# A two-layer transformer trunk on one core: the ungated half of the gating layer as seven block products, weight sums by VectorE and by accumulating loads, the second gate block by weight rows

## The chip, the cores and the metric

The kernel runs on one core of a Trainium2 chip. The metric is the device time of one execution in microseconds (us). Before the change three runs gave 1406.53, 1407.19 and 1410.97 us, with a median of 1407.19 us. The engines are named as in the profile: PE (TensorE, matmuls; PEld its weight loads), DVE (VectorE), ACT (ScalarE), POOL (GpSimd) and SP (SyncE, which here only issues transfers).

## The reference, cut to what matters

The input is 512 tokens of width 1024, all in float32. Layer 0 is a chunked attention, layer 1 a gating layer, and each is followed by an MLP. What the change touches is the gating layer and the second product of both MLPs:

```python
def chunked_spatial_gating(h, w_in, v_gain, w_s, b_s, w_out):
    z = jax.nn.gelu(h @ w_in, approximate=False)          # 512x1024 @ 1024x6144
    u, v = jnp.split(z, 2, axis=-1)                       # 512x3072 each
    v = rms_norm(v, v_gain).reshape(B, nw, 128, 8, 384)
    w = jnp.where(mask[None], w_s, 0.0)                   # 8 groups of 128x128
    vm = jnp.einsum('gij,bnjgc->bnigc', w, v) + b_s.T[None, None, :, :, None]
    return (u * vm.reshape(B, S, 3072)) @ w_out           # 512x3072 @ 3072x1024

def squared_relu_mlp(h, w1, w2):
    return jnp.square(jax.nn.relu(h @ w1)) @ w2           # 1024 -> 4096 -> 1024
```

The norm of v needs its sum of squares over all 3072 columns, so no tile can be mixed and gated before the whole gated half v is there.

## The kernel before, in words

A float32 matrix is held as a high and a low part (`Split`, lines 480 to 484: a CAST on ACT at L483 and a subtraction on DVE at L484), and a product is three matmuls, high by high, high by low and low by high (`mm3`, L94; each matmul is recorded at L92). A matmul here takes a 128x128 block as its weights and streams 512 columns of the other matrix into one PSUM bank. Tokens come in four tiles of 128.

Some of the large products are made by a scheme of seven block products (`seven`, L616). Left matrix and weights are cut in 2x2 blocks, 256 tokens by 512 and 512 by 512, and seven products of sums of blocks stand in for eight plain ones. The sums of weight blocks are made on DVE at L631 on whole 512x512 blocks of two 128x1024 tiles; the sums of left blocks at L530; each finished product is added to its output by `put` (for the MLP at L517 and L519, for the gated half at L1425 and L1423). Four weight blocks are loaded per scheme. `Run` (L687) puts the steps in a row: a step's loads are issued `ll` steps and its weight split `lp` steps before its matmuls, (3, 3) in the MLPs and (2, 2) in the gating layer, where a step is 24 matmuls.

The scheme is used three times in each MLP's second product (the last quarter of the 4096 hidden columns is plain, in `project_last`) and twice in the gated half v: columns 0 to 511 (`gate_tile(0, ...)`) and 512 to 1023 (`gate_tile(1, ...)`, the second plain block) are plain, columns 1024 to 3071 are two schemes with `Gate` as output. The finished v goes to DRAM (`v_store`, L1400, issued on POOL) and is loaded again later (`v_load`, L1405).

The ungated half u is plain. `u_block(cb)` (L1518) makes 512 columns for all four token tiles: 24 matmuls a tile, gelu at L1531, v scaled by its row norm and gain at L1533, split at L1535 and L1536, mixed with the 128x128 group matrices by three short matmuls for each group, shifted and multiplied with u at L1549, turned by four 128x128 transposes at L1554 and split again into high and low at L1559 and L1560. Six such blocks alternate with `b_down`, which multiplies a finished block of 512 columns with its rows of `w_out` (96 matmuls, with `wload`, L379, whose split is at L388 and L389) and adds the result to `y` at L517. The last two blocks go through `project_last`, which also adds the residual and starts the norm of the MLP that follows. There `merge` (L498) multiplies y by the adaLN gate at L506, loads the residual `xs` again and adds it at L507.

Pieces of work for later stages (`bg`: rows of the adaLN modulation, mostly L194 on DVE) are spread over the stages by a counter. Buffers are 49 slots of 128x1024 float32 and 8 PSUM banks, handed out in the order in which they came free. Inside `in_order` the code's order is PE's order; outside it a scheduler sets the order on every engine from its own estimate of durations, and each engine then works strictly in its order.

## Time and profile before

| quantity | value |
|---|---|
| median of three runs | 1407.19 us (1406.53 to 1410.97) |
| the profiled execution | 1412.96 us |
| its span, first to last instruction | 1411.2 us |
| busy PE / DVE / ACT / POOL | 1386.7 / 1020.9 / 713.5 / 15.7 us |
| mean granted TensorE clock | 0.993 |

The profile is of one execution. Its span is 1.8 us shorter than its time, and that time is 5.8 us above the median. Busy means that an instruction is on the engine. A busy PE may still be slower than it could be, because matmuls overlap; the pace is read from the number of matmuls that a long stretch holds. An engine's idle time is put down to what ended it.

### The profile page before, as it was taken

Reading aid. Unit: us, or ns where it says so; the run is one execution under the profiler, and the core shown is the slowest. Engines: PE = TensorE matmul, PEld = TensorE weight load, DVE = VectorE, ACT = ScalarE, POOL = GpSimd, SP = SyncE. Lnnn points to the kernel's source line nnn. Section 1 sums busy time; section 2 is a strip of 40 time slices with the busy share of each in tenths; the row PEclk is TensorE's granted clock in tenths of the full one; section 3 lists DMA queues with packets and bytes.
Section 4 is the critical chain, followed back from the end, with each engine's and each line's share of the span. In section 5 each row is a group of like instructions: output and inputs, shape, how many; then the busy total and the mean of one; then the engine's idle time right before and its main releaser. Section 6 shows DMA issues by size and latency. Waiting matters only on the chain.

```text
span 1411.2 us, 18916 instructions
## 1 busy us (share of the span) xinstructions
PE 1386.7 (98%) x7202; PEld 1185.5 (84%) x7202; DVE 1020.9 (72%) x1493; ACT 713.5 (51%) x1231; POOL 15.7 (1%) x46
## 2 busy tenths in 40 slices
PE   8999999899999999999999999999999999999998
PEld 7898888789888888888888888888889988888887
DVE  6889889676667887776995745665677377776883
ACT  6537567655464544537587443233445355453630
POOL 0000000000000000000000000000000000000000
PEclk8999999999999999999999999999999999999999
DMA  9656466573254361356347434435437225242151
GB/s 373 240 144 211 147 194 173 201 264 110 90 169 144 119 224 60 118 197 252 134 147 254 167 106 164 163 127 164 142 113 269 75 87 182 63 147 90 31 164 60
DMA packets 85627, 221.51 MB, mean 157 GB/s; under 512 B 7960, under 2 KB 9376, under 8 KB 85536
## 3 DMA queue, kind: packets, MB, share of 16 engines
q1 hardware_dynamic: 83808, 214.01, 45.9%
q0 software_dynamic: 1728, 6.29, 1.1%
q8 instruction: 56, 0.92, 0.3%
q14 instruction: 35, 0.29, 0.1%
HBM read 197.21 MB, written 14.68 MB: 150 GB/s over the span
## 4 chain that ended last, share of the span: by engine, by line
PE 88%; DMA 6%; DVE 3%; ACT 2%; issue 1%; SPq 0%; POOL 0%; ACTq 0%; POOLq 0%; DVEq 0%
PE p L92 85%; DMA s<-in_ada_w 2%; DMA s<-in_ffn_w 1%; DMA s<-in_a_w_in 1%; DMA s<-in_a_w_out 1%; DMA s<-s 1%; PE p L1554 1%; PE p L1228 1%; PE p L315 1%; DVE s L484 0%; PE p L1139 0%; PE p L920 0%; DVE s L951 0%; ACT s L483 0%; PE p L207 0%
## 5 line engine op out<-in xcount | busy, mean ns | idle before, releaser
L92 PE MATMUL p<-s,s 128*128 128x512 f32 (+2 forms) x6568 | 1323.8, 361 | 9.5 <-DVE nm L1190 2.7
L92 PEld LDWEIGHTS p<-s,s 128*128 128x128 f32 x6568 | 1109.4, 189 | 196.0 <-DVE nm L1190 4.3
L484 DVE TENSOR_TENSOR s<-s,s 128x1024 fp32r<-128x1024 f32 x234 | 280.5, 1222 | 119.1 <-ACT s L483 56.0
L483 ACT CAST s<-s 128x1024 fp32r<-128x1024 f32 x234 | 241.2, 1051 | 166.0 <-PE p L92 109.9
L389 DVE TENSOR_TENSOR s<-s,s 128x1024 fp32r<-128x1024 f32 x80 | 96.7, 1223 | 62.2 <-ACT s L388 50.7
L388 ACT CAST s<-s 128x1024 fp32r<-128x1024 f32 x80 | 83.4, 1052 | 93.8 <-DMA s<-in_b_w_out 34.1
L631 DVE TENSOR_TENSOR s<-s,s 128x1024 f32<-128x1024 f32 x64 | 77.7, 1222 | 33.0 <-DMA s<-in_ffn_w 32.6
L739 ACT ACTIVATE r<-p 128x512 f32<-128x512 f32 x64 | 38.1, 595 | 116.6 <-PE p L92 116.5
L194 DVE SCALAR_TENSOR_TENSOR s<-s,cs,s 128x1024 f32<-128x1024 f32 x70 | 89.7, 1281 | 8.7 <-DMA s<-in_ada_w 7.7
L517 DVE TENSOR_TENSOR s<-p,s 128x512 f32<-128x512 f32 x104 | 70.4, 686 | 19.2 <-PE p L92 18.0
L745 ACT ACTIVATE s<-r 128x256 f32<-128x256 f32 (+1 forms) x112 | 45.0, 443 | 1.2
L424 DVE TENSOR_TENSOR tr<-p,s 128x512 f32<-128x512 f32 (+1 forms) x33 | 22.0, 671 | 30.6 <-PE p L92 30.2
L1195 ACT ACTIVATE s<-s,nm 128x128 f32<-128x128 f32 (+3 forms) x64 | 36.0, 564 | 7.4 <-DVE nm L1190 5.9
L1559 ACT CAST s<-p 128x256 fp32r<-128x256 f32 x48 | 17.7, 370 | 35.5 <-PE p L1554 27.0
L530 DVE TENSOR_TENSOR s<-s,s 128x1024 f32<-128x1024 f32 x28 | 33.6, 1221 | 1.0 <-PE p L92 0.9
L304 ACT ACTIVATE s<-s 128x512 f32<-128x512 f32 x24 | 15.3, 638 | 36.0 <-DVE s L425 34.9
L1233 DVE TENSOR_TENSOR s<-p,s 128x512 fp32r<-128x512 f32 (+3 forms) x64 | 29.3, 484 | 4.0 <-ACT s L1232 3.6
L1560 DVE TENSOR_TENSOR s<-p,s 128x256 fp32r<-128x256 f32 x48 | 20.1, 419 | 16.3 <-ACT s L1559 16.3
L1190 DVE CUSTOM_DVE_ANT_0 s<-p,s 128x128 f32<-128x128 f32 (+3 forms) x64 | 29.6, 485 | 0.9 <-PE p L92 0.8
L1535 ACT CAST s<-s 128x512 fp32r<-128x512 f32 x24 | 14.8, 621 | 27.8 <-DVE s L1533 12.9
L1228 PE MATMUL p<-ident,s 128*128 128x128 f32 x160 | 24.6, 275 | 4.1 <-ACT sq L1310 2.4
L1232 ACT CAST s<-p 128x512 fp32r<-128x512 f32 (+3 forms) x64 | 25.1, 426 | 6.6 <-PE p L1228 5.5
(141 smaller groups left out, 760.9 us busy)
## 6 DMA issues: line engine op xcount, KB each, us to landing
s<-in_ffn_w SPq DMA_DIRECT2D x128, 512.0 KB, 4.5
s<-in_ada_w SPq DMA_DIRECT2D x96, 512.0 KB, 4.9
s<-in_b_w_in SPq DMA_DIRECT2D x48, 512.0 KB, 5.0
s<-in_b_w_out SPq DMA_DIRECT2D x24, 512.0 KB, 4.8
s<-in_a_w_in SPq DMA_DIRECT2D x22, 512.0 KB, 5.2
s<-s SPq DMA_DIRECT2D x64, 128.0 KB, 3.6
vd<-s POOLq DMA_DIRECT2D x12, 512.0 KB, 3.2
s<-vd SPq DMA_DIRECT2D x12, 512.0 KB, 3.4
```

The costliest lines, as they stand in the source:

```text
L92: T.matmul(ps, lhsT, rhs, start=start, stop=stop, skip_group_check=more)
L194: V.scalar_tensor_tensor(acc, r, ck, acc, ALU.mult, ALU.add)
L388: A.copy(hi, raw)
L389: engs[len(ids) // 2 % len(engs)].tensor_tensor(lo, raw, f32(hi), ALU.subtract)
L483: A.copy(self.hi, raw)
L484: mark[0] = V.tensor_tensor(self.lo, raw, f32(self.hi), ALU.subtract)
L517: V.tensor_tensor(dst, ps, dst, ALU.add)
L631: V.tensor_tensor(x[0], y_[0], z[0], ALU.subtract)
L739: A.activation(r, ps, AF.Relu)
L745: A.activation(d, v, AF.Square)
L1195: A.activation(pt[it], pt[it], AF.Exp, bias=nm[:, it:it + 1], scale=-1.0, accum_out=sm[:, it:it + 1])
L1228: T.transpose(ps[:, it * P:(it + 1) * P], b["pt"][it][:, jt * P:(jt + 1) * P], ident)
```

## The change

Five things change.

1. `seven` works in half blocks of weights (256 rows, one 128x1024 tile), so that a scheme is 14 steps of 12 matmuls instead of 7 of 24, and it uses other sums: per scheme seven partial results are put instead of eight, one of them in one go from PSUM (`whole`). Where `near` is false (the MLPs) all sums of weight blocks are made by loads that add (`grow`: a transfer issued on POOL with accumulation, into the tile that held the block before); three blocks are loaded plainly and four are added. Where `near` is true (the gating layer) two sums are made by DVE (`plus`, L628 of the changed kernel) and two by adding loads, and four blocks are loaded plainly.
2. The ungated half u is made by three such schemes (`mix_steps`), 1024 columns each, with `Mix` as output. The mixing and gating of a tile is queued and comes out two steps after its last product (five at the first). The gated tile is turned as before, copied to a full-precision tile, and split in whole 512x256 blocks (`take_parts`).
3. The first 2048 rows of the output product are two plain products of 1024 rows (`down_steps`), walked through by rows of the weights, 24 matmuls a step. The order is u0, down0, u1, u2, down1, and then `project_last` as before.
4. The second plain block of the gated half is four steps of 256 weight rows (`gate_steps`) instead of four token tiles.
5. The row norms of v come from an integer estimate with three refinements on DVE instead of a function on ACT; v is stored by transfers issued on ACT; the last residual is added to y by an adding load on POOL instead of a load and a sum on DVE; `Run` is (4, 4) in the MLPs and (4, 3) in the gating layer, in the smaller steps.

```diff
 
-        def merge(self, xs, g):
...
                 xt[t], xid[t] = self.y[t], self.ids[t]
+                if late:
+                    V.tensor_tensor(xt[t], xt[t], g, ALU.mult)
+                    G.dma_start(xt[t], xs[t], accum_op=ALU.add)
+                    return
                 raw, done = raw_tile([P, D])
                 SP.dma_start(raw, xs[t])
...
             if (t, hf) in self.seen:
-                V.tensor_tensor(dst, ps, dst, ALU.add)
+                V.tensor_tensor(dst, dst, ps, op)
             else:
                 A.copy(dst, ps)
                 self.seen.add((t, hf))
...
-    def seven(left, src, y):
+    def seven(left, src, y, near=False):
+
...
+        def load(name, i, j, s_):
+            raw[name, s_] = t, n = SL.get([P, 2, 512], F32)
+            SP.dma_start(t, block(i, j, s_))
+
+        def grow(i, j, name, s_):
+            G.dma_start(raw[name, s_][0], block(i, j, s_), accum_op=ALU.add)
+
+        def plus(a, b, s_):
+            V.tensor_tensor(raw[a, s_][0], raw[a, s_][0], raw[b, s_][0], ALU.add)
+
+        def right(m, name, add, s_):
+
+            if near and m == 2:
+                plus("x", "w", s_)
+                SL.free(raw["w", s_][1])
+            op[m, s_] = Split(raw[name, s_][0], [P, 2, 512])
+            if near and m == 4:
+                plus("x", "y", s_)
+            if add is None:
+                SL.free(raw[name, s_][1])
+            elif not near or m > 2:
+                grow(*add, name, s_)
+
+        def mult(m, acc, first, outs, done, s_):
+            a, b = left.op[m], op.pop((m, s_))
             for u in range(2):
-                if first:
+                if first and s_ == 0:
...
-                for k in range(4):
-                    bh, bl = b[k // 2].hi[:, k % 2, :], b[k // 2].lo[:, k % 2, :]
-                    mm3(p, a.hi[:, k, c], a.lo[:, k, c], bh, bl, first and k == 0, k == 3, not first)
-                for i, j in outs:
...
+                for k in range(2):
+                    kk = 2 * s_ + k
+                    ah, al, bh, bl = a.hi[:, kk, c], a.lo[:, kk, c], b.hi[:, k, :], b.lo[:, k, :]
+                    mm3(p, ah, al, bh, bl, first and kk == 0, kk == 3, not first)
+                if s_:
+                    for i, j, o, whole in outs:
+                        y.put(2 * i + u, j, p, o, whole)
+                    if done:
+                        PS.free(pi)
+            b.free()
+            if s_:
+                left.done(m)
...
         plan = (
-            (True, ((0, 0),), False),
-            (True, ((0, 0),), True),
-            (True, ((1, 1),), False),
-            (False, ((0, 1),), False),
-            (False, ((0, 1),), True),
-            (False, ((1, 0), (1, 1)), True),
-            (True, ((1, 0),), True),
+            (0, ("x", 0, 0), ("x", (0, 1)), ("z", True, ((0, 0, add, False),), False)),
+            (1, ("z", 1, 0), ("z", None), ("y", True, ((0, 0, add, False),), True)),
+            (2, None, ("x", (1, 1)), ("v", True, ((1, 1, add, False),), False)),
+            (4, ("y", 1, 1), ("y", (0, 1)), ("v", False, ((0, 1, add, False),), True)),
+            (3, None, ("x", (1, 0)), ("z", False, ((0, 1, sub, False),), False)),
+            (5, None, ("y", None), ("z", False, ((1, 1, sub, False),), False)),
+            (6, None, ("x", None), ("z", False, ((1, 0, add, True),), True)),
...
+        def loads(m, b, s_):
+            if near and m == 2:
+                load("w", 0, 1, s_)
+            if b:
+                load(*b, s_)
+
...
     def v_store(cb, b):
 
         v, i = vv.pop((cb, b))
-        G.dma_start(vd[cb, b], v.rearrange("p t n -> p (t n)"))
+        A.dma_start(vd[cb, b], v.rearrange("p t n -> p (t n)"))
...
+    def gate_steps(cb):
...
     def gate_load(cb):
         return wload(b_w_in[0][:, SGH + cb * 512:SGH + cb * 512 + 512], KD)
 
-    steps = []
+    steps = gate_steps(1)
     for p in (1, 2):
-        steps += seven(kept, b_w_in[0][:, SGH + p * 1024:SGH + (p + 1) * 1024], Gate(p))
-    u_ahead = []
-    steps.append(Step(nothing, lambda: u_ahead.append(wload(b_w_in[0][:, 0:512], KD)), nothing, nothing))
...
+    class Mix:
...
+        def put(self, t, hf, ps, op, whole):
+            if (hf, t // 2) not in self.u:
+                self.u[hf, t // 2] = SL.get([P, 2, 512], F32)
+            dst = self.u[hf, t // 2][0][:, t % 2, :]
+            if not whole and (t, hf) not in self.seen:
+                self.seen.add((t, hf))
+                A.copy(dst, ps)
+                return
+            if not whole:
+                V.tensor_tensor(dst, dst, ps, op)
+            A.activation(dst, ps if whole else dst, AF.Gelu)
+            late = 5 if (self.p, hf, t // 2) == (0, 0, 0) else 2
+            later.append((now[0] + late, lambda: self.mix(t, hf, dst)))
+        def mix(self, t, hf, u):
+            cb = 2 * self.p + hf
+            vh = tp.tile([P, 512], F32, tag="tt", name="vh")
+            v, vi = self.v[hf, t // 2]
+            V.scalar_tensor_tensor(
+                vh, v[:, t % 2, :], vr[:, t:t + 1], self.g[:, hf * 512:hf * 512 + 512], ALU.mult, ALU.mult
+            )
+            vs, i = SL.get([P, 2, 512], F32R)
+            A.copy(vs[:, 0, :], vh)
+            V.tensor_tensor(vs[:, 1, :], vh, f32(vs[:, 0, :]), ALU.subtract)
+            ps, pi = bank()
+            c0 = 0
...
+                mark[0] = V.scalar_tensor_tensor(
+                    u[:, c0:c1], ps[:, c0:c1], bsT[:, g:g + 1], u[:, c0:c1], ALU.add, ALU.mult
+                )
...
+    def mix_steps(p):
+        m = Mix(p)
+        out = seven(kept, b_w_in[0][:, p * 1024:(p + 1) * 1024], m, True)
+        out[0].right = then(out[0].right, m.gain, lambda: m.take(0, 0))
+        for i, hf, b in ((6, 1, 0), (8, 1, 1), (10, 0, 1)):
+            out[i].right = then(out[i].right, lambda hf=hf, b=b: m.take(hf, b))
+        return out
+    def down_steps(p):
...
+        def mult(n):
+            hf, j, o = n // 4, 1 - n // 2 % 2, n % 2
+            w = op.pop(n)
+            for t in range(NT):
+                if n % 4 == 0:
+                    ps[t] = bank()
+                a = parts[p, t // 2, j]
+                c = slice(t % 2 * P, t % 2 * P + P)
+                for k in range(2):
+                    kk = 2 * o + k
+                    mm3(
+                        ps[t][0], a.hi[:, kk, c], a.lo[:, kk, c], w.hi[:, k, :], w.lo[:, k, :],
+                        n % 4 == 0 and k == 0, n % 4 == 3 and k == 1,
+                    )
+                if n % 4 == 3:
+                    y.put(t, hf, ps[t][0])
+                    PS.free(ps[t][1])
+            w.free()
+            if n in (5, 7):
+                for i in range(2):
+                    parts.pop((p, i, j)).free()
+            bg((0, 2, 2, 1, 1, 1, 1, 1)[n])
...
+    steps[3].mult = then(steps[3].mult, mixing)
+    steps[-1].mult = then(steps[-1].mult, row_scales)
...
+    u, d = [mix_steps(p) for p in range(3)], [down_steps(p) for p in range(2)]
+    tail = [Step(nothing, down_ahead, nothing, nothing)]
+    for x in u[0] + u[1] + u[2] + d[0] + d[1]:
+        x.mult = then(x.mult, flush)
+    for x, *f in (
+        (u[0][13], take(0, 1)), (d[0][1], take(0, 0)), (u[1][13], last_use), (u[2][11], take(1, 1)),
+        (u[2][13], take(1, 0)), (d[1][1], no_more_mixing), (d[1][4], take(2, 0)), (d[1][5], take(2, 1)),
+    ):
+        x.mult = then(x.mult, *f)
+    steps += u[0] + d[0] + u[1] + u[2] + d[1][:6] + tail + d[1][6:]
...
-        run = Run(steps, 3, 3)
+        run = Run(steps, 4, 4)
...
-    run = Run(steps, 2, 2)
-    run.go()
-    h = kept.only_blocks()
+    run = Run(steps, 4, 3)
+    with tc.issue_after(normed[0].ins):
+        run.prime()
+    keep[0] = 9
+    run.go()
...
-
-    u_block(0)
-    u_block(1)
-    b_down([0])
-    u_block(2)
-    b_down([1])
-    u_block(3)
-    b_down([2])
-    u_block(4)
-    b_down([3])
-    u_block(5)
-    kept.free()
-    SL.free(*[i for _, i in wsT])
-    b_down([4, 5])
+    in_order()
+    g = gbc[1, 2][0]
+    project_last(
+        plain({(i, j): parts[2, i, j] for i in range(2) for j in range(2)}), b_w_out[0][2048:3072, :], g,
+        last.rows, last.cols, lambda: up_ahead(1), y.merge(xs, g, True), spent
+    )
```

On PE, in the middle of the ungated half, before the change: `p_369` and `p_372` are token tiles of a u block, `s_925` is a gated tile being turned, `p_370` is a mixing result, and `s_701` to `s_716` are weights of the block.

```order
L92 MATMUL p_369_8209<-s_917_8143,s_702_6415 128x512
L92 MATMUL p_369_8209<-s_918_8144,s_702_6415 128x512
L92 MATMUL p_369_8209<-s_917_8143,s_703_6416 128x512
L1554 MATMUL p_368_8197<-ident,s_925_8182 128x128
L92 MATMUL p_369_8209<-s_917_8143,s_702_6415 128x512
L92 MATMUL p_369_8209<-s_918_8144,s_702_6415 128x512
L1554 MATMUL p_368_8197<-ident,s_925_8182 128x128 x3
L92 MATMUL p_369_8209<-s_917_8143,s_703_6416 128x512
L92 MATMUL p_370_8240<-s_929_8237,s_841_7498 128x128 x3
L92 MATMUL p_370_8240<-s_929_8237,s_841_7498 128x384 x3
L92 MATMUL p_372_8261<-s_908_8125,s_712_6601 128x512
```

The same place after it: `p_357` and `p_356` are accumulators of one scheme, `p_374` is the first product of the next scheme, and `s_971` is a gated tile.

```order
L92 MATMUL p_357_8295<-s_973_8490,s_779_7038 128x512
L92 MATMUL p_357_8295<-s_974_8491,s_779_7038 128x512
L1602 MATMUL p_369_8581<-ident,s_971_8479 128x128 x2
L1602 MATMUL p_367_8560<-ident,s_971_8479 128x128 x4
L1602 MATMUL p_369_8581<-ident,s_971_8479 128x128 x2
L92 MATMUL p_357_8295<-s_973_8490,s_780_7039 128x512
L92 MATMUL p_374_8699<-s_985_8589,s_694_6389 128x512
```

Before, a tile's 24 matmuls, one transposed tile and one mixing follow each other; now two gated tiles are turned together at the end of a run of matmuls, between the products of two schemes.

On DVE at the same place, before: L389 splits weights, L1560 splits gated tiles, L1549 gates.

```order
L389 TENSOR_TENSOR s_938_8366<-s_936_8363,s_937_8365 128x1024
L1560 TENSOR_TENSOR s_922_8154<-p_368_8197,s_921_8153 128x2x128
L1549 SCALAR_TENSOR_TENSOR s_928_8234<-p_370_8240,bsT,s_928_8234 128x128
L1549 SCALAR_TENSOR_TENSOR s_928_8234<-p_370_8240,bsT,s_928_8234 128x384
L1560 TENSOR_TENSOR s_924_8156<-p_368_8197,s_923_8155 128x2x128
L389 TENSOR_TENSOR s_941_8372<-s_939_8369,s_940_8371 128x1024
```

And after: L628 is the sum of two weight half blocks, L486 the split, L1568 the sum of a product into u, L1595 the gating, L1582 and L1577 the split and the scaling of v.

```order
L628 TENSOR_TENSOR s_967_8465<-s_967_8465,s_984_8587 128x1024
L486 TENSOR_TENSOR s_991_8616<-s_972_8488,s_990_8615 128x1024
L1568 TENSOR_TENSOR s_964_8439<-s_964_8439,p_356_8288 128x512
L1595 SCALAR_TENSOR_TENSOR s_964_8439<-p_370_8636,bsT,s_964_8439 128x384
L1595 SCALAR_TENSOR_TENSOR s_964_8439<-p_370_8636,bsT,s_964_8439 128x128
L1568 TENSOR_TENSOR s_964_8439<-s_964_8439,p_357_8295 128x512
L628 TENSOR_TENSOR s_972_8488<-s_972_8488,s_989_8613 128x1024
L1582 TENSOR_TENSOR s_994_8654<-vh,s_994_8654 128x512
L1577 SCALAR_TENSOR_TENSOR vh<-s_970_8471,vr,s_935_8167 128x512
```

The splits of gated tiles in quarters are gone from between the gating; weight sums and the sums of products into u now stand between the instructions of the mixing.

## Rows read from the trace of the kernel before

**Rows 1.** The page: busy time of the engines in us with the share of the span and the number of instructions, the granted clock in 40 slices of the span, and the chain that ended last by engine.

```profile
PE 1386.7 (98%) x7202; PEld 1185.5 (84%) x7202; DVE 1020.9 (72%) x1493; ACT 713.5 (51%) x1231; POOL 15.7 (1%) x46
...
PEclk8999999999999999999999999999999999999999
...
PE 88%; DMA 6%; DVE 3%; ACT 2%; issue 1%; SPq 0%; POOL 0%; ACTq 0%; POOLq 0%; DVEq 0%
```

**Rows 2.** Busy time in four stretches (us from the span's start): first the length, then busy us and instructions of PE, PEld, DVE, ACT and POOL, then granted clock, DMA share and GB/s.

```profile
700.00:750.00 50.00, 50.00 (x222) 41.30 (x221) 46.30 (x47) 40.39 (x66) 2.96 (x6) 1.00 0.46 153
779.00:1021.00 242.00, 242.00 (x1175) 203.23 (x1174) 149.64 (x227) 87.32 (x140) 0.00 (x0) 1.00 0.44 147
1021.00:1083.20 62.20, 60.42 (x334) 52.02 (x333) 46.34 (x81) 30.48 (x65) 0.00 (x0) 1.00 0.58 206
1083.20:1407.40 324.20, 324.20 (x1588) 275.09 (x1587) 212.41 (x215) 142.02 (x197) 0.00 (x0) 1.00 0.32 101
```

**Rows 3.** PE's groups by shape from 1300 to 1400 us: count, busy us, mean ns of one, idle time before them. Then the first group over the whole span.

```profile
L92 PE MATMUL p<-s,s 128*128 128x512 f32 x439 | 100.1, 389 | 0.0
L92 PE MATMUL p<-s,ones 128*128 128x512 f32 x4 | 1.3, 396 | 0.0
...
L92 PE MATMUL p<-s,s 128*128 128x512 f32 x4648 | 1084.1, 392 | 5.3 <-ACT s L1272 2.1 <-DVE nm L1190 1.4 <-ACT s L980 1.0
```

**Rows 4.** PE in order of time around 812 us: start, length, and what (lengths overlap; the pace is from start to start).

```profile
811.64 0.60 PE L1554 MATMUL p<-ident,s 128*128 128x128 f32 x4
812.00 1.17 PE L92 MATMUL p<-s,s 128*128 128x512 f32 x4
```

**Rows 5.** DVE's groups by shape (count, busy us, mean ns, idle before them): the first two over the whole span, the others from 779 to 1021 us.

```profile
L484 DVE TENSOR_TENSOR s<-s,s 128x1024 fp32r<-128x1024 f32 x234 | 280.5, 1222 | 119.1 <-ACT s L483 56.0 <-PE p L92 52.8 <-issue 4.5
L631 DVE TENSOR_TENSOR s<-s,s 128x1024 f32<-128x1024 f32 x64 | 77.7, 1222 | 33.0 <-DMA s<-in_ffn_w 32.6
...
L194 DVE SCALAR_TENSOR_TENSOR s<-s,cs,s 128x1024 f32<-128x1024 f32 x14 | 17.9, 1282 | 2.8 <-DMA s<-in_ada_w 2.5
L1536 DVE TENSOR_TENSOR s<-s,s 128x512 fp32r<-128x512 f32 x24 | 16.3, 687 | 1.9 <-ACT s L1535 1.7
L517 DVE TENSOR_TENSOR s<-p,s 128x512 f32<-128x512 f32 x24 | 16.2, 685 | 5.2 <-PE p L92 5.2
L1533 DVE SCALAR_TENSOR_TENSOR s<-s,vr,gain 128x512 f32<-128x512 f32 x20 | 14.9, 748 | 14.4 <-PE p L92 11.1 <-issue 1.4 <-PE p L1554 1.1
...
L1549 DVE SCALAR_TENSOR_TENSOR s<-p,bsT,s 128x384 f32<-128x384 f32 x15 | 9.1, 609 | 0.0
L1549 DVE SCALAR_TENSOR_TENSOR s<-p,bsT,s 128x256 f32<-128x256 f32 x16 | 7.0, 479 | 1.0 <-PE p L92 0.8
L1549 DVE SCALAR_TENSOR_TENSOR s<-p,bsT,s 128x128 f32<-128x128 f32 x15 | 5.2, 344 | 0.9 <-PE p L92 0.9
```

**Rows 6.** Transfers. For L625 (half blocks of weights for the schemes), L1400 (stores of v, issued on POOL) and L1405 (their loads back): the issue with its length in ns, least, median and most, and the time to landing. Then the stores of the same size issued on SP, with KB and median us to landing.

```profile
L625 SPq DMA_DIRECT2D s<-in_b_w_in x16: 367/373/642, 619.1 to 719.6; - x16
DMA to landing us min/median/max: 3.4/4.6/11.7
...
L1400 POOL DMA_DIRECT2D vd<-s x12: 531/531/673, 663.0 to 772.2; - x12
DMA to landing us min/median/max: 2.9/3.2/7.6
...
L1405 SPq DMA_DIRECT2D s<-vd x12: 326/338/459, 745.4 to 964.0; - x12
DMA to landing us min/median/max: 3.1/3.4/7.9
...
xs<-s SPq DMA_DIRECT2D x8, 512.0 KB, 2.9
...
xsg<-s SPq DMA_DIRECT2D x4, 512.0 KB, 2.6
```

**Rows 7.** ACT's groups by shape: the first over the whole span, the others from 779 to 1021 us.

```profile
L483 ACT CAST s<-s 128x1024 fp32r<-128x1024 f32 x234 | 241.2, 1051 | 166.0 <-PE p L92 109.9 <-DMA s<-in_ffn_w 28.2 <-DVE s L484 12.6
...
L1531 ACT ACTIVATE s<-p 128x512 f32<-128x512 f32 x24 | 14.4, 600 | 25.7 <-PE p L92 25.7
L1535 ACT CAST s<-s 128x512 fp32r<-128x512 f32 x23 | 14.2, 622 | 27.8 <-DVE s L1533 12.9 <-PE p L92 12.7 <-DVE s L389 2.0
L519 ACT COPY s<-p 128x512 f32<-128x512 f32 x8 | 4.7, 589 | 8.4 <-PE p L92 8.4
```

**Rows 8.** The page: packets and bytes of all transfers.

```profile
DMA packets 85627, 221.51 MB, mean 157 GB/s; under 512 B 7960, under 2 KB 9376, under 8 KB 85536
```

**Rows 9.** The chain that ended last, at the change to the last MLP: start, length, what.

```profile
1019.14 4.40 DMA s<-in_ffn_w
...
1067.88 10.67 DMA s<-in_ffn_w
```

More of the change, by code (lines that the diff above doesn't have):

```diff
@@ L584, in comb @@
             super().comb(d, a, b, o)
+        more = True
         def done(self, m):
-            pass
-        def only_blocks(self):
-            for m in (2, 3, 4, 5):
-                self.op.pop(m).free()
-            return self.rows()
-        def free(self):
-            for x in self.op.values():
-                x.free()
+            if not self.more:
+                super().done(m)
     def plain(p):
@@ L677, in seven @@
+        def loads(m, b, s_):
[3 more added lines that the diff above has]
+                load(*b, s_)
         return [
             Step(
-                (lambda m=m: load(*blocks[m])) if m < 4 else nothing,
-                lambda m=m: right(m),
-                lambda m=m: left.prep(m),
-                lambda m=m: mult(m, *plan[m]),
+                lambda m=m, b=b, s_=s_: loads(m, b, s_),
+                lambda m=m, r=r, s_=s_: right(m, *r, s_),
+                lambda m=m, s_=s_: prep(m, s_),
+                lambda m=m, p=p, s_=s_: mult(m, *p, s_),
@@ L683, in seven @@
             )
-            for m in range(7)
+            for m, b, r, p in plan for s_ in range(2)
         ]
@@ new lines, in then, with both, take_parts @@
+    def then(f, *gs):
+        def both():
+            f()
+            for g in gs:
+                g()
+        return both
+    y = Sum()
+    parts = {}
+    def take_parts(*blocks):
+        for b in blocks:
+            t, n = gated.pop(b)
+            parts[b] = Split(t, [P, 4, 256])
+            SL.free(n)
+    def mix_steps(p):
[5 more added lines that the diff above has]
+        return out
@@ new lines, in trunk_kernel, with down_ahead, last_use, no_more_mixing @@
+    steps[3].mult = then(steps[3].mult, mixing)
+    steps[-1].mult = then(steps[-1].mult, row_scales)
+    def down_ahead():
+        ahead[0] = wload(b_w_out[0][2048:3072, 0:512], KD)
+    def last_use():
+        kept.more = False
+    def no_more_mixing():
+        SL.free(*[i for _, i in wsT])
+    def take(p, j):
+        return lambda: take_parts(*[(p, i, j) for i in range(2)])
+    u, d = [mix_steps(p) for p in range(3)], [down_steps(p) for p in range(2)]
+    tail = [Step(nothing, down_ahead, nothing, nothing)]
```

328 lines of the change are left out of this document (159 added, 169 removed).

## The prediction

> **What bounds the kernel now.** I read the page first. PE is busy for 98% of the span, DVE for 72%, ACT for 51%, POOL for almost nothing, and PE's lines take 88% of the chain that ended last [rows 1]. The granted clock is full in all slices but the first. So the first question is how many matmuls there are. Then I read windows by stage, since busy shares say nothing of the place: from 700 to 750 us (the two schemes of the gated half) and from 779 to 1021 us (the ungated half and most of the output product) PE is never idle [rows 2]; it has idle time, 1.8 us of 62.2, only at the change to the next MLP, 1021 to 1083 us. Because matmuls overlap, "busy" is no proof of full pace, so I counted: 100 us late in the last MLP hold 439 + 4 matmuls of 512 columns, 0.2257 us each [rows 3]; the 50 us of [rows 2] hold 222, which is the same pace. The reader is to see that in the stage that changes most, PE is the limit, and that in the densest window DVE was busy for 46.30 of 50 us and PE still did not wait.
>
> **The matmuls.** The ungated half takes 6 blocks x 4 token tiles x 24 = 576 matmuls of 512 columns now. Three schemes take 3 x 7 products x 2 token tiles x 12 = 504. Everything else on PE keeps its number: the plain part of the output product has 4 x 96 = 2 x 192, the second gate block 96, mixing and transposes the same. So 72 go, at 0.2257 us: **-16.25 us**. They stand in a stretch where PE is the limit, so I count all of it, less what is late next.
>
> **What is late next: DVE in a u scheme.** PE needs 168 x 0.2257 = 37.9 us for its products. Beside it stand eight mixings, which stream three times 512 columns (3 x 0.2257 = 0.68 us), and eight groups of four transposes, 812.00 - 811.64 = 0.36 us each [rows 4]: 8.3 us, together 46.2 us. DVE has, by [rows 5]: 14 weight splits and 4 weight sums at 1.222 (22.0 us); 6 sums of a product into u at 0.685 (4.1); for each of 8 tiles 0.748 for scaling v, 0.687 for its split and 0.609 + 0.344 or 2 x 0.479, so 0.955, for gating (19.1). That is 45.2 us of 46.2, a load of 98%. The schemes u1 and u2 stand in a row, and four gated blocks are split while u2 runs (4 x 1.222 = 4.9): DVE has 95.3 us of work where PE has 92.4. I take the difference, **+2.9 us**. The lower end is 0: the down stages before and after have 8 splits (9.8), at most 8 sums (5.5) and some ten pieces of modulation at 1.28 (L194) beside 192 x 0.2257 = 43.3 us of PE, some 15 us free, into which mixings and splits can move. The upper end: if DVE can be no busier than in the densest window, 92.6%, each scheme lasts 45.2 / 0.926 = 48.8 us, three times 2.6 more, and the four splits 5.3: 13.1 us. I stay near the low end since that window, the nearest row, shows no wait of PE at 93%.
>
> **The adding loads.** The trace has none. The nearest rows are a plain load of the same half block of weights, 4.6 us to landing, a store of such a tile from POOL, 3.2 us, and its load back, 3.4 us [rows 6]. An adding load can't be quicker than the plain one, and if it went like load, read and write in turn it took 4.6 + 3.2 + 3.4 = 11.2 us. I take the plain load and one read of the tile, 7.8 us. The room for it: in the gating layer four steps of 12 matmuls (2.71 us) lie between the split of a tile and the next split of it, 10.8 us, and a split stands three steps ahead of its matmuls, 8.1 us. From 18.9 us go the issue on POOL (0.53), the CAST (1.05) and the subtraction (1.22) of the split [rows 5 to 7], so 16.1 us are left: nothing waits at 7.8 or at 11.2. In an MLP two steps of 24 matmuls lie between as well, and the split is four steps ahead: at least 21.7 + 10.8 - 2.8 = 29.7 us. So 0, and the risk is a rival below. A plain load's slowest landing is 11.7 us, which still fits. POOL gets 72 such issues, 72 x 0.53 = 38 us spread over some 1000.
>
> What speaks against this: the twelve stores issued on POOL landed in 3.2 us at the median, 7.6 at most, while stores of the same size issued on SP took 2.9 and 2.6 [rows 6]; so issuing on POOL cost 0.3 to 0.6 us beside a DVE that was over 90% busy. The Trainium skill says more (SBUF — State Buffer, section "SBUF: two separate sides"): POOL writes the descriptors of its transfers into SBUF itself, and some DVE operations lock it out until they end. By that rule a load would start one DVE operation, 1.22 us, later, or several where they follow without a gap, as in the u schemes. The trace agrees only with the small end. One operation changes no sum, several in a row are what could make the second rival true.
>
> **The rest, each at nothing.** In the MLPs a scheme loses 8 weight sums on DVE (9.8 us) and two sums of results; PE is the limit there too [rows 2], so it gives nothing, and if the cover were gone it would be a gain. The splits of gated tiles at L1559 and L1560 become one copy and whole splits. ACT per u scheme: 14 x 1.05 + 6 x 0.589 + 8 x 0.600 + 8 x (0.622 + 0.589) = 32.7 of 46.2 us [rows 7]; the stores of v that move to ACT's queue add 12 issues of 0.34 us (as SP's loads of v take, [rows 6]). The row norms of v by some 15 short DVE operations are needed only five steps (13.5 us) after the first tile. The last residual: y is scaled (1.22), the adding load is issued (0.53) and lands (7.8 to 11.2), 9.6 to 13.0 us after y; DVE wants it after 42 matmuls and 8 transposes, 10.2 us, and PE only with the transposes another 36 matmuls on. The second gate block by weight rows has the same work. Weights to be loaded grow by 18 blocks of 1.05 MB in the MLPs and 10 in the gating layer, 29 MB on 221.51 [rows 8], 13%, with the DMA engines half idle in these windows. The 1.8 us at the change to the MLP are waits for its weights [rows 9] and stay, within 2 us either way.
>
> **Sum.** The profiled execution took 1412.96 us (span 1411.2 and 1.8 around it): 1412.96 - 16.25 + 2.9 = 1399.6. The median is 5.8 us lower, so **1394 us**.
>
> **Rivals.** First, DVE sets the pace of the u schemes. For it: 98% load, and mixing is a chain DVE-ACT-DVE-PE-DVE-PE in strict queues. Against it: [rows 2]. Price 13.1 instead of 2.9: 1404 us. Second, and slower than before: adding loads land late and splits wait for them on ACT, with evictions and gelu queued behind, for which PE's banks wait. It decides from 16.1 + 13.4 / 5 = 18.8 us to landing, where the five schemes of the gating layer have given back the gain. At twice my upper bound, 22.4 us, each scheme waits 6.3 us, 31.5 in all: 1425 us. For it: nothing in the trace shows an accumulation; against it: 18.8 us is over four plain loads. Third, the change doesn't do what it says: half-size steps double the number of steps, and if PE loses 0.1 us at each of the 70 + 84 steps, 15 us, the time is 1409 with the 2.9. For it: each step waits for its own split; against it: in [rows 4] PE passes from one tile to another without a loss.
>
> **How the numbers follow.** A measurement of this kernel can tell about 0.3%, 4.2 us, from no change: faster is below 1403.0, slower above 1411.4. Forecast 0.60, its own range 1389 (no wait, 1.8 us gained at the change to the MLP) to 1400, all faster. DVE's pace 0.20: 0.10 faster, 0.08 same, 0.02 slower. Late adding loads 0.12: 0.10 slower, 0.02 same. Lost pace 0.08: 0.05 same, 0.03 slower. Together 0.70, 0.15, 0.15. The range that leaves out 2 in 10 is 1388 to 1410.
>
> **What would show it.** PE's 512-column matmuls go from 4648 to 4576 in the group by shape [rows 3], still at about 222 in 50 us. In the u schemes DVE is over 90% busy and PE waits, if at all, for the DVE lines of gating or splits, 3 us in sum. Adding loads land in under 12 us, and ACT's casts do not wait for them. In the MLPs DVE is less busy and PE as full. I am wrong if PE waits more than 8 us between the gate and the next MLP, or if casts wait for weight transfers issued on POOL.

## The result and the profile after

The changed kernel takes 1413.38 us (median of 20 runs, 1408.14 to 1418.41), the kernel before 1408.67 us beside it (20 runs). The ratio is 1.0037, interval 1.0027 to 1.0047: slower, by about as much as can be told from no change, where I had forecast 1394 us. The profiled execution of after took 1416.04 us.

The page of after: busy time, and the chain that ended last by engine and by line. They answer to [rows 1].

```profile
PE 1378.7 (97%) x7130; PEld 1177.0 (83%) x7130; DVE 978.7 (69%) x1422; ACT 744.0 (53%) x1248; POOL 95.0 (7%) x106
...
PE 74%; issue 11%; DMA 7%; DVE 6%; ACT 2%; POOL 0%; SPq 0%; POOLq 0%; DVEq 0%; ACTq 0%
PE p L92 71%; DMA s<-in_b_w_in 2%; DMA vd<-s 1%; DMA s<-xsg 1%; DVE s L958 1%; PE p L1235 1%; DVE s L486 1%; DVE s L1197 1%; DMA s<-s 1%; ACT s L485 1%; DVE s L1240 0%; PE p L1602 0%; DMA s<-in_ada_w 0%; PE p L315 0%; DMA s<-in_x 0%
```

PE has less work and a smaller share of the span, and DVE is less busy than before. In the chain PE fell from 88% to 74%; "issue" has 11% where it had 1, and by line the first thing behind PE is the transfer of weights of the gating layer. Two rows of PE's groups by shape follow, first over the whole span, then from 1300 to 1400 us, to be held against [rows 3].

```profile
L92 PE MATMUL p<-s,s 128*128 128x512 f32 x4576 | 1075.0, 394 | 13.9 <-ACT s L1565 3.6 <-ACT s L1279 2.3 <-DVE s L486 2.2
...
L92 PE MATMUL p<-s,s 128*128 128x512 f32 x439 | 99.8, 389 | 0.0
```

The 72 matmuls are gone, and the pace late in the last MLP is the same to the matmul. So the loss must stand in some stretch. Busy time of after by 25 us (length, then PE, PEld, DVE, ACT, POOL, granted clock, DMA share, GB/s):

```profile
700.00:725.00 25.00, 22.61 (x97) 17.99 (x96) 19.83 (x20) 16.17 (x23) 2.41 (x2) 0.98 0.94 251
725.00:750.00 25.00, 25.00 (x107) 20.60 (x106) 14.76 (x16) 14.20 (x26) 3.61 (x3) 0.95 0.49 120
750.00:775.00 25.00, 23.14 (x94) 18.40 (x93) 14.56 (x14) 14.90 (x24) 1.21 (x1) 0.93 0.92 290
775.00:800.00 25.00, 21.36 (x92) 17.28 (x91) 16.00 (x30) 15.17 (x25) 3.61 (x3) 0.98 0.70 182
800.00:825.00 25.00, 24.19 (x123) 20.55 (x122) 21.32 (x32) 16.22 (x24) 1.20 (x1) 0.95 0.54 146
...
950.00:975.00 25.00, 21.60 (x91) 17.90 (x90) 18.14 (x23) 16.76 (x23) 0.00 (x0) 0.86 0.53 139
...
779.00:1021.00 242.00, 234.15 (x1115) 196.03 (x1114) 185.12 (x240) 132.46 (x184) 14.46 (x12) 0.98 0.61 176
```

Where [rows 2] showed PE busy without a gap at full clock, from the gated half to the output product, it now stops in five of these stretches, and the clock is below full in all six. The waits of PE from 690 to 1000 us (what waited for what, us in total, times, longest):

```profile
PE p L92 <- ACT s L1565: 3.6, 1, 3.6
PE p L92 <- ACT s L1581: 3.4, 2, 2.7
PE p L92 <- DVE s L486: 2.2, 1, 2.2
PE p L92 <- ACT s L485: 1.8, 1, 1.8
PE p L1602 <- DVE s L1595: 0.8, 1, 0.8
```

They add up to 11.8 us. The clock of the six stretches lacks 0.02 + 0.05 + 0.07 + 0.02 + 0.05 + 0.14 = 0.35 of 25 us, 8.8 us. Together 20.6 us against a gain of 16.25: by this estimate the execution should be 4.3 us longer than the 1412.96 of before, and it is 3.1.

DVE is not what PE waits for in the first place, and it was itself idle. What ACT waited for explains more. Two views of line L625 in after from 690 to 1000 us: the adding loads of weights, their issue on POOL (ns, least, median, most), who waited for them, and the time to landing.

```profile
L625 POOL DMA_DIRECT2D s<-in_b_w_in x20: 1203/1203/1467, 695.9 to 946.1; - x20
...
who waited for it (us, times):
  ACT s L485: 34.0, 13
...
DMA to landing us min/median/max: 6.0/8.2/14.5
```

Against [rows 6]: the landing is close to what I took (8.2, taken 7.8), the issue more than twice as long (1.20, taken 0.53), and casts wait for 13 of the 20. One such place in full, the end of the second u scheme: first POOL's issues, then ACT, then PE in order of time (start, length, what, idle time before it and what ended it).

```profile
941.35 2.44 POOL L625 DMA_DIRECT2D s<-in_b_w_in  x2 [49.77 <-ACT s L1565]
944.16 1.20 POOL L625 DMA_DIRECT2D s<-in_b_w_in  x1 [0.38 <-DVE s L486]
946.14 1.20 POOL L625 DMA_DIRECT2D s<-in_b_w_in  x1 [0.77 <-DVE s L486]
```

```profile
947.60 1.05 ACT L485 CAST s<-s 128x1024 fp32r<-128x1024 f32 x1 [3.02 <-DMA s<-in_b_w_in]
...
952.23 1.05 ACT L485 CAST s<-s 128x1024 fp32r<-128x1024 f32 x1 [1.95 <-DMA s<-in_b_w_in]
956.93 1.04 ACT L485 CAST s<-s 128x1024 fp32r<-128x1024 f32 x1 [3.65 <-DMA s<-in_b_w_in]
957.89 0.61 ACT L1581 CAST s<-vh 128x512 fp32r<-128x512 f32 x1
958.41 0.58 ACT L1565 COPY s<-p 128x512 f32<-128x512 f32 x1
958.88 0.62 ACT L1581 CAST s<-vh 128x512 fp32r<-128x512 f32 x1
960.70 2.00 ACT L485 CAST s<-s 128x1024 fp32r<-128x1024 f32 x2 [1.20 <-DMA s<-in_b_w_in]
```

```profile
949.41 6.42 PE L92 MATMUL p<-s,s 128*128 128x512 f32 x27
958.55 0.33 PE L92 MATMUL p<-s,s 128*128 128x128 f32 x1 [2.72 <-ACT s L1581]
959.55 10.56 PE L92 MATMUL p<-s,s 128*128 128x128 f32 x35 [0.68 <-ACT s L1581]
```

Four adding loads, four casts that wait for them, 9.8 us. The first cast is wanted at 947.60 - 3.02 = 944.58, 3.2 us after the issue of its load began. Behind the third stand two casts of scaled v (L1581), with the eviction of a product (L1565) between them, in ACT's strict order, and both stops of PE end with such a cast of v. The last row shows the second price: 35 matmuls, some of them short, take 10.56 us, 0.30 us each, where one of 512 columns took 0.2257 in [rows 3].

The landing is counted from the start of the issue: the last load was issued at 946.14 and landed 14.5 us later, the longest of the 20, and its cast starts at 960.70. The four casts start 3.8 to 4.7 us apart, each as its load lands, and the DMA engines were full meanwhile (DMA share, the last number but one, 0.89 to 1.12 in every 3 us from 943 to 961 us; two of these windows):

```profile
949.00:952.00 3.00, 3.00 (x16) 2.50 (x15) 0.92 (x1) 1.21 (x3) 0.00 (x0) 1.00 1.12 207
952.00:955.00 3.00, 3.00 (x15) 2.45 (x15) 1.23 (x1) 1.05 (x1) 0.00 (x0) 1.00 1.11 257
```

So at this place the later ones shared full engines with the loads before them.

### The profile page after: what moved, and what is told of

It is laid out like the page before. It is cut to its first block, busy times and chain, and to the rows that moved or that the text cites. A ratio compares the mean times of both kernels' runs of the same rounds, so it can differ in the third digit from the quotient of the medians.

```text
span 1414.3 us, 18911 instructions
## 1 busy us (share of the span) xinstructions
PE 1378.7 (97%) x7130; PEld 1177.0 (83%) x7130; DVE 978.7 (69%) x1422; ACT 744.0 (53%) x1248; POOL 95.0 (7%) x106
## 4 chain that ended last, share of the span: by engine, by line
PE 74%; issue 11%; DMA 7%; DVE 6%; ACT 2%; POOL 0%; SPq 0%; POOLq 0%; DVEq 0%; ACTq 0%
PE p L92 71%; DMA s<-in_b_w_in 2%; DMA vd<-s 1%; DMA s<-xsg 1%; DVE s L958 1%; PE p L1235 1%; DVE s L486 1%; DVE s L1197 1%; DMA s<-s 1%; ACT s L485 1%; DVE s L1240 0%; PE p L1602 0%; DMA s<-in_ada_w 0%; PE p L315 0%; DMA s<-in_x 0%
## 5 line engine op out<-in xcount | busy, mean ns | idle before, releaser
L486 DVE TENSOR_TENSOR s<-s,s 128x1024 fp32r<-128x1024 f32 x308 | 371.3, 1223 | 231.7 <-ACT s L485 181.0
L485 ACT CAST s<-s 128x1024 fp32r<-128x1024 f32 x308 | 316.6, 1050 | 227.4 <-PE p L92 101.5
L625 POOL DMA_DIRECT2D s<-in_ffn_w x48 | 58.3, 1215 | 498.7 <-DVE s L486 395.1
L523 DVE TENSOR_TENSOR s<-s,p 128x512 f32<-128x512 f32 x76 | 50.4, 683 | 16.6 <-PE p L92 16.3
L388 ACT CAST s<-s 128x1024 fp32r<-128x1024 f32 x36 | 37.5, 1049 | 36.4 <-DMA s<-in_ffn_w 18.3
L389 DVE TENSOR_TENSOR s<-s,s 128x1024 fp32r<-128x1024 f32 x36 | 43.4, 1222 | 10.4 <-ACT s L388 10.1
L536 DVE TENSOR_TENSOR s<-s,s 128x1024 f32<-128x1024 f32 x28 | 33.6, 1223 | 10.9 <-PE p L92 10.5
L625 POOL DMA_DIRECT2D s<-in_b_w_in x20 | 24.1, 1218 | 234.6 <-DVE s L486 165.1
L319 ACT ACTIVATE tt<-p,mod,mod 128x128 f32<-128x128 f32 x64 | 24.0, 464 | 20.9 <-PE p L315 10.4
L304 ACT ACTIVATE s<-s 128x512 f32<-128x512 f32 x24 | 15.3, 638 | 34.8 <-DVE s L425 33.7
L425 DVE TENSOR_TENSOR s<-s,tr 128x512 f32<-128x512 f32 (+1 forms) x33 | 22.2, 674 | 15.4 <-DMA s<-xsg 14.7
```

Source lines behind the costliest of these rows:

```text
L388: A.copy(hi, raw)
L389: engs[len(ids) // 2 % len(engs)].tensor_tensor(lo, raw, f32(hi), ALU.subtract)
L485: A.copy(self.hi, raw)
L486: mark[0] = V.tensor_tensor(self.lo, raw, f32(self.hi), ALU.subtract)
L523: V.tensor_tensor(dst, dst, ps, op)
L625: G.dma_start(raw[name, s_][0], block(i, j, s_), accum_op=ALU.add)
```

## The experiments

Theory A: the adding loads land later than the casts want them, and what stands behind those casts on ACT stops PE. Theory B: plain loads or the stores of v are late, not the adding loads. Theory C: adding loads take the DMA engines' time from other transfers. And the first rival of the prediction: DVE.

Ratios are to runs of the kernel before on the same chip.

| run | median us | ratio to before, 95% interval |
|---|---|---|
| after | 1413.38 | 1.0037 (1.0027 to 1.0047) |
| e1: all sums on DVE | 1405.34 | 0.9977 (0.9965 to 0.9989) |
| e2: plain loads for adding loads | 1398.43 | 0.9924 (0.9910 to 0.9937) |
| e3: split a step earlier, load as before | 1426.16 | 1.0124 (1.0106 to 1.0143) |
| e4: stores of v on SP | 1412.75 | 1.0028 (1.0018 to 1.0037) |
| e5: gated half on DVE | 1405.02 | 0.9974 (0.9965 to 0.9983) |
| e6: sums on POOL | 1419.84 | 1.0075 (1.0059 to 1.0091) |
| e7: e5, u with one adding load of two | 1403.86 | 0.9962 (0.9947 to 0.9976) |
| e8: plain loads a step earlier | 1412.42 | 1.0020 (1.0008 to 1.0032) |
| e9: early adding loads | 1402.26 | 0.9947 (0.9935 to 0.9960) |
| e10: gated half on DVE, early ones in u | 1396.16 | 0.9914 (0.9897 to 0.9930) |
| e11: e10, plain loads in the MLPs | 1396.05 | 0.9902 (0.9885 to 0.9919) |
| e12: e10, residual merged as before | 1394.21 | 0.9897 (0.9877 to 0.9917) |

**e1, all sums on DVE.** The half blocks 01 and 10 stay in their tiles, and DVE adds them where the adding load was.

```diff
+            if near == "dve" and m in (3, 4):
+                o = {4: "w", 3: "z"}[m]
+                plus(name, o, s_)
+                SL.free(raw[o, s_][1])
```

> All four weight sums of the five schemes of the gating layer are made by DVE from half blocks that stay in their tiles; no adding load is left there (the MLPs keep theirs). Theory A (a cast waits for an adding load, everything behind it on ACT is late, PE stops and then runs at a lower clock): the some 12 us of stops of PE between 700 and 985 us and the fall of the granted clock there go, some 20 us; DVE gets 4.9 us more per scheme, which in a u scheme is 50.1 us beside 46.2 of PE, so up to 12 us come back: 1394 to 1406 us. Theory B (the stops come from the burst of plain loads and of the stores of v, whose slots are taken again at once): the stops stay and DVE's load is added: 1413 to 1425 us.

1405.34 us, as theory A said. From 700 to 775 us PE now stops for 0.4 us only; nearly all that is left stands in the u schemes and waits for DVE, which has too much to do there. PE's waits from 690 to 1000 us:

```profile
PE p L92 <- DVE s L1575: 3.7, 1, 3.7
PE p L1609 <- DVE s L1602: 1.6, 1, 1.6
...
```

With two smaller ones they come to 7.0 us. That is the rival "DVE sets the pace", brought about by 4.9 us more per scheme.

**e2, plain loads in place of adding loads.**

```diff
-            G.dma_start(raw[name, s_][0], block(i, j, s_), accum_op=ALU.add)
+            if near:
+                G.dma_start(raw[name, s_][0], block(i, j, s_))
+            else:
+                G.dma_start(raw[name, s_][0], block(i, j, s_), accum_op=ALU.add)
```

> The adding loads of the gating layer become plain loads of the same bytes, issued by POOL at the same place with the same waits; the sums of those weights are left out, so the values are others. Theory A in the form that the accumulation itself is what is late (1.20 us of issue and 8.2 us to landing, where a plain load has 0.53 and 4.6): the stops of PE go from some 12 to under 4 us, 1396 to 1402 us. If instead any load between the two splits of one tile is too late here, or under theory B, it stays at 1410 to 1415 us.

1398.43 us, 15.0 below after and 10.2 below the kernel before, where 13.4 were forecast, with the same waits, the same bytes and the same issuing engine; PE's stops fall to 3.4 us. So the accumulation is the price. The same view as above:

```profile
L626 POOL DMA_DIRECT2D s<-in_b_w_in x20: 722/722/753, 695.4 to 933.4; - x20
...
who waited for it (us, times):
  ACT s L485: 8.0, 7
...
DMA to landing us min/median/max: 3.9/5.1/8.6
```

Accumulating adds 0.48 us to the issue on POOL and 3.1 us to the landing, which includes the issue. In the same stretch the 10.49 MB of POOL's queue took 10.4% of the DMA engines' time in e2 and 20.4% in after, so the engines, too, work twice as long for an added byte; theory C stays possible up to here.

**e3 and e8, other leads.** `Run(steps, 4, 3)` becomes `Run(steps, 3, 4)`, and `Run(steps, 5, 3)`.

> In the gating layer weights are loaded three steps ahead of their split and split four steps ahead of their matmuls (four and three before): a late split has 2.7 us more before PE needs it, the room between the two splits of a tile stays four steps. Theory A: PE's stops shrink by 2.7 us each, most go, 1397 to 1406 us. Theory B (loads and slots): plain loads have 2.7 us less before their split, casts wait more for them, 1412 to 1418 us.

> In the gating layer every plain load of weights is asked for one step (2.7 us) earlier; split and matmuls as they were, the room of the adding loads too. Theory A (adding loads): within 2 us of 1413. Theory B (plain loads are late, as splitting one step earlier with loads one step nearer made it 13 us slower): 1400 to 1408 us.

e3 missed both theories: 13 us slower than after, with 19.3 us of PE's waits from 690 to 1000 us instead of 11.8. Casts waited 26.3 us for adding loads and 4.3 us for plain ones, so plain loads did not become the late ones, and a longer lead of the split did not help. What makes it worse than after stays open. A lack of free tiles is one candidate, not shown: its longest stop, 4.4 us near 766 us, is for an eviction (L1430) that had waited 4.6 us for a store of v, a wait that this line does not have in after. e8 moved the time by nothing (intervals overlap): plain loads were not late either. Theory B falls for after, with **e4**:

```diff
-        A.dma_start(vd[cb, b], v.rearrange("p t n -> p (t n)"))
+        SP.dma_start(vd[cb, b], v.rearrange("p t n -> p (t n)"))
```

> The twelve stores of v are issued on SP instead of ACT. Theory A: nothing changes, 1411 to 1416 us. Theory B, that issues of stores on ACT's queue or the waits of casts for them (9.1 us in the gate) make ACT late: up to 9 us less, 1404 to 1409 us; if SP's loads of weights are held up behind the stores, 1415 to 1422 us.

1412.75 us, no difference from after.

**e5 and e7, which half pays.** e5 has e1's edit in the gated half alone; e7 also lets DVE make the sum 11 + 01 in the u schemes, so that one adding load of two is left.

> DVE makes all four weight sums in the two schemes of the gated half (it has 32.3 us of work beside 37.9 of PE there); the u schemes keep their two adding loads. Theory A1 (the accumulation is late in both halves, about 15 us in all, of which the gate has the larger share by the stops of PE, 7.7 of some 12 us before 800 us): 1400 to 1406 us, below the version with DVE in all five schemes if DVE's load costs more in a u scheme than two late adding loads. Theory A2 (the u schemes have most of it): 1407 to 1412 us.

> Gate schemes with all sums on DVE; in the u schemes DVE makes three sums, and one adding load (four in a row of half steps later it is split) is left of two. DVE has 47.7 us there beside 46.2 of PE. Theory A1 with DVE at the edge: between the version with both adding loads in u and the one with none, 1398 to 1405 us. Rival: the adding load that is left is the late one: as with both, within 1 us.

1405.02 and 1403.86 us. The gated half pays 8 us of the 15, as theory A1 had it, which leaves some 7 to the u schemes. e7 is not told from e5, so neither its theory nor its rival is decided. What is left in e7 is mixed: PE waits for DVE (6.8 us from 690 to 1000 us), and casts wait 5.0 us for the adding loads that are left.

**e6, the sums on POOL.** In e1's kernel `V.tensor_tensor` becomes `G.tensor_tensor` for the two sums that adding loads made in after.

> POOL makes the two sums that the adding loads made, in all five schemes, from half blocks that stay in their tiles; DVE keeps its two. Theory A (what counts is how soon the sum is there): if POOL needs under 4 us for a sum (a POOL copy or sum of this size is not in the traces; DVE has 1.22), it is there sooner than an adding load with 1.20 + 8.2 us, and DVE has no more to do: 1396 to 1403 us. Rival: POOL is slower than 5 us a sum, or slows DVE's operations beside it: 1410 to 1425 us.

1419.84 us: the rival was right. The sum on POOL and a sum on DVE (both at one line, 690 to 1000 us):

```profile
L630 POOL TENSOR_TENSOR s<-s,s x20: 2393/2408/6657, 695.9 to 954.2; 128x1024 f32<-128x1024 f32 x20
L630 DVE TENSOR_TENSOR s<-s,s x17: 1211/1222/3298, 711.8 to 945.5; 128x1024 f32<-128x1024 f32 x17
```

A sum takes 2.4 us on POOL at the median, but up to 6.7, and DVE's own of 1.22 us up to 3.3: the two slow each other down. Of DVE's splits and weight sums from 690 to 1000 us, the 91 with no POOL sum beside them took 1.23 us at most; the 18 with one took up to 3.4.

**e9, the same number of adding loads with room.** The adding loads make the two sums that need nothing computed, 00 + 01 and 11 + 01, in fresh tiles that are asked for four half steps before a plain load would be; DVE's two sums are 00 + 01 + 11 and that + 10.

```diff
+        own = {"dve": (3, 4), "pool": (3, 4), "mix": (4,), "early": (3,)}.get(near, ())
...
+                name = {2: "s", 3: "s", 5: "t", 6: "s"}.get(m, name)
...
+                plus("s" if near == "early" else "x", "y", s_)
...
+            elif m in own:
+                o = {4: "w", 3: "z"}[m]
+                plus(name, o, s_)
...
+            if near == "early" and m in (0, 4):
+                o, i = {0: ("s", 0), 4: ("t", 1)}[m]
+                load(o, i, i, s_)
+                grow(0, 1, o, s_)
```

> As many adding loads in the gating layer (20) and as many sums by DVE (20), but the adding loads make the two sums that need no earlier operand: half block 00 + 01 and 11 + 01, each into a fresh tile that is loaded plainly and then added to, asked for four half steps before a plain load would be; DVE makes 00 + 01 + 11 and adds 10 to it. Two plain loads of 0.5 MB more and two fewer adding waits per half block; room from issue to the cast at least 21.7 us less the plain landing (5 us). Theory A (the adding load's 1.2 + 8.2 us do not fit into the four half steps between two casts of one tile, for want of room): casts no longer wait, 1396 to 1402 us, as the version with plain loads in place of adding loads. Theory C (adding loads take the DMA engines' time from the other transfers, wherever they stand): 1408 to 1416 us.

1402.26 us, just above what theory A expected and well below theory C, although the layer now loads more: 58 plain loads of weights instead of 48. The expectation counted two more for each half of a scheme, and it is one. The adding loads of e9, 690 to 1000 us:

```profile
  ACT s L485: 2.5, 2
...
DMA to landing us min/median/max: 6.0/8.9/10.7
```

They land no sooner, and ACT waits 2.5 us for them instead of 34.0. What decides is how early they are issued before the cast that wants them. The 4 us by which e9 stays above e2 may be a part of theory C (eight plain loads more in this stretch, and twice the engines' time for each added byte) or lie ahead of the gating layer, as the next run suggests; no run separates them.

**e10, and the price of the rest.** e5's gated half with e9's u schemes.

> The same early adding loads in the u schemes alone, all sums of the gated half on DVE (no adding load there). Theory A: within 2 us of the version with early adding loads everywhere, 1396 to 1402 us, 3 to 9 us below the version with DVE in the gated half and late adding loads in u. Theory C: as that version, 1403 to 1408 us, and below the one with early adding loads everywhere by some 7 us.

1396.16 us, 13.6 below the 1409.78 of the kernel before in those runs, and faster than both kernels. Busy time by stretch, with the window of [rows 2]:

```profile
925.00:950.00 25.00, 25.00 (x123) 21.00 (x122) 23.92 (x31) 18.91 (x26) 0.00 (x0) 1.00 0.44 146
...
779.00:1021.00 242.00, 240.95 (x1170) 201.90 (x1169) 193.79 (x258) 127.93 (x178) 11.22 (x10) 1.00 0.58 178
```

The clock is full again, and DVE is busy for 96% of the stretch shown, late in the u schemes; PE's waits from 690 to 1000 us are three, 1.0 us in sum, all for DVE. Theory A had it 3 to 9 us below e5, which it is (8.9), and within 2 us of e9, which it is not (6.1). But that difference is mostly not the gated half: of the 7.3 us between the spans of the two profiled executions, 5.5 are there before the first gelu of the gating layer, where the two have the same code. A measure of the layer itself is the time from that first gelu to the last one of u, here in e10 (line and operation, count, ns least, median, most, start of the first and of the last):

```profile
L1471 ACT ACTIVATE s<-p x8: 587/598/598, 651.5 to 690.3; 128x512 f32<-128x512 f32 x8
...
L1588 ACT ACTIVATE s<-p x6: 584/607/629, 807.3 to 963.0; 128x512 f32<-128x512 f32 x6
```

and in after:

```profile
L1452 ACT ACTIVATE s<-p x8: 590/600/612, 654.0 to 692.9; 128x512 f32<-128x512 f32 x8
...
L1569 ACT ACTIVATE s<-p x6: 592/597/602, 827.2 to 981.3; 128x512 f32<-128x512 f32 x6
```

311.5 us in e10, 327.3 in after: 15.8 us of the 22.4 between the two profiled executions (17.2 between the medians). By the same two lines e5 has 317.2, e9 313.0 and e2 308.2. The next two runs have e10's code in this layer, and there it takes 316.6 and 310.8 us: one execution tells such a time to some 6 us only, so after stands apart, and e9 is not told from e10.

e11 lets the MLPs load plainly, and e12 sets `y.merge(xs, g)` for `y.merge(xs, g, True)`.

> The version with DVE's sums in the gated half and early adding loads in the u schemes; beside that the 48 adding loads of the two MLPs become plain loads of the same bytes from POOL (those weight sums are left out). The prediction's step that adding loads cost nothing in an MLP: within 2 us of that version, 1394 to 1398 us. If they cost there what they cost in the gating layer (15 us for 20): 1360 to 1385 us.

> The same version with the residual of the gating layer merged as before the change (plain load of it by SP and a second sum on DVE, no adding load). The prediction's step that the adding load of the residual is worth nothing: within 2 us, 1394 to 1398 us. If DVE's waits for it (14.7 us in three waits at the change to the MLP) were what ends last there: up to 4 us less.

Both are within 2 us of e10, and their intervals overlap with it: the 48 adding loads of the MLPs and the residual's are worth nothing that can be measured. The landing of those 48 in after, and of the plain loads in their place in e11 (KB each, median us to landing):

```profile
s<-in_ffn_w POOLq DMA_DIRECT2D x48, 512.0 KB, 5.9
...
s<-in_ffn_w POOLq DMA_DIRECT2D x48, 512.0 KB, 4.2
```

An adding load of the same size lands after 5.9 us there, not 8.2: what it takes depends on the place.

## Why the prediction was wrong

**The matmuls, right.** 4576 of 512 columns, at the pace of before. Where the late adding loads of the gating layer are gone the gain comes: e10 is 13.6 us and e12 15.3 us below the kernel before of the same runs; I had 16.25 - 2.9 = 13.4.

**DVE in a u scheme, right.** I took 2.9 us, 0 to 13.1. In e10, with DVE's count as I had it, PE waits 1.0 us for DVE. In after DVE was below 90% in the u schemes, against what I had listed, for it waited itself, for ACT's casts. e1 shows where the edge is: with 50.1 us of DVE beside 46.2 of PE its waits are 7.0 us.

**The adding loads, wrong, and in one term: the room.** The landing was near what I took in the gating layer at the median (7.8 taken, 8.2 measured), partly by luck, since the same load took 5.9 us in the MLPs; its longest, 14.5 us, is above the 12 that I gave as a sign, and the issue was 1.20 us, not 0.53, which was a store's. But "16.1 us are left" counted the three steps by which a split stands ahead of its matmuls (8.1 us) as room. They are room for that product only. On ACT the cast for a later step stands ahead of what PE needs at the step at hand, as the rows from 956.93 to 958.88 show, so a cast that waits holds that up. Of PE's 11.8 us of stops 7.0 were for pieces right behind a cast that had waited for an adding load (L1565, L1581), and 4.0 for late splits themselves (L485, L486).

What is left are the four steps between two casts of a tile, 10.8 us, less the first cast and subtraction (1.05 + 1.22): as an estimate 8.5 us from the start of the issue, and 6.1 to 7.3 where another issue on POOL (1.20), a sum on DVE (1.22) or both stand ahead. (The prediction took the load's own issue off as well, though the landing includes it.) The traces show less than this estimate: at the 13 casts that waited, the time from the start of the issue to the moment when ACT stood ready, read as at the place shown, was 3.1 to 3.6 us in five, 5.0 at the median, and up to 13.4 where earlier waits had already put the cast off. What narrows it beyond the estimate stays open. A plain load with 5.1 us mostly fits (in e2 ACT waited 8.0 us in seven casts, and PE stopped for 3.4), an adding load with 8.2 does not.

The second rival, with a chance of 0.12, was the right one, and I had its queue right. Its point of decision, 18.8 us, carried the same 8.1 us: without them it is 10.7, and with the 5.0 us of the casts that waited 5.0 + 13.4 / 5 = 7.7 us, an estimate that lies below the 8.2 measured. Both of the prediction's own signs of being wrong came: PE's stops went over 8 us, and casts waited for POOL's loads.

**The clock, missing.** The sum priced waits at their length. In after's execution the lost clock of the six stretches comes to three quarters of PE's stops (8.8 us to 11.8).

**The rule on SBUF's sides, without weight here.** In e2, beside a DVE at least as busy as in after (242 and 225 us of 310), plain loads from POOL landed in 5.1 us and from SP in 4.7 us at the median, and POOL's issue was 722 ns nearly every time. Of the 0.4 us between them 0.35 is the longer issue (0.72 against 0.37 us). So what the Trainium skill says of POOL's descriptors and DVE (SBUF — State Buffer, "SBUF: two separate sides") shows next to nothing in these runs; the 3.1 us are the accumulation's. The section names DVE operations in a two-port mode, and ones with two inputs in SBUF only against a POOL operation that reads SBUF. The splits and sums of 1.22 us have two inputs in SBUF, so the prediction's "one DVE operation, 1.22 us, later" took more from it than it says. POOL does read SBUF in e6, and there such sums of DVE went from 1.22 to as much as 3.3 us.

**At nothing, right:** the MLPs (e11, and 222 matmuls in 50 us), the residual (e12), the stores on ACT (e4). At the change to the MLP PE was idle 1.2 us of 66 (1.8 before, [rows 2]). The third rival, pace lost at half steps, has nothing for it: from 825 to 950 us PE is never idle, and from 400 to 500 us, in an MLP whose schemes also go by half steps, it made 447 matmuls before and after.

## What to carry to other kernels

Where engines work strictly in order, the room of a transfer that waits for an earlier use of its tile is the distance between two uses in the queue of the engine that uses it, less the work on the tile in between. The lead by which results are prepared is not room; it hides lateness only if nothing urgent stands behind. Give an accumulating load a fresh tile and an operand that needs nothing computed, and it can be issued as early as there are tiles free, at the cost of more plain loads (58 for 48 in e9). Price a stop of PE at more than its length.

## What the runs showed of the hardware

- An accumulating load of 0.5 MB from POOL: issue 1.20 us (plain 0.72), landing from the start of the issue 8.2 us at the median in the gating layer (plain 5.1, e2) and 5.9 in the MLPs (plain 4.2, e11), twice the DMA engines' time for the same bytes (20.4% against 10.4% of the stretch for 10.49 MB). Four of them within 4.8 us filled the engines, and the last landed after 14.5 us.
- After PE had stopped for 2.72 and 0.68 us the granted clock was at the lower level, 1.2 GHz of 2.4, for several microseconds (granted clock in windows of 3 us, after):

```profile
955.00:958.00 3.00, 0.83 (x4) 0.37 (x2) 0.00 (x0) 1.06 (x2) 0.00 (x0) 1.00 1.08 254
958.00:961.00 3.00, 1.77 (x6) 1.58 (x7) 2.99 (x5) 1.80 (x4) 0.00 (x0) 0.74 0.97 322
961.00:964.00 3.00, 3.00 (x11) 2.81 (x10) 2.92 (x5) 3.00 (x4) 0.00 (x0) 0.50 0.03 10
964.00:967.00 3.00, 3.00 (x10) 2.28 (x10) 3.00 (x5) 3.00 (x5) 0.00 (x0) 0.62 0.01 3
```

- Element-wise sums on POOL and DVE at the same time stretch each other (e6): 2.4 to 6.7 us on POOL; on DVE 1.22 to 3.3 us, with the weight splits at 1385 ns on average from 690 to 985 us in e6 where they take 1222 in after.
